# First block: token-major norm sums, another order between a stage's last product and the next norm, conditioning steps moved

## The chip, the cores and the metric

One core of a Trainium2 chip runs the whole program: two transformer blocks after each other on 256 tokens (272 with 16 meta tokens). The metric is the device time of one execution in microseconds (us), the median of the runs; lower is better.

## The reference, cut to what matters

The first block has two layers, each a mixing stage and a conv FFN; the residual h is kept, and the output of each stage is normalised before it is added:

```python
for l in range(DEPTH):                               # first block, DEPTH = 2
    u = _rms_norm(h, norm_mix_pre[l])
    ...
    h = h + _rms_norm(merged @ w_out[l], norm_mix_post[l])
    f = _conv_ffn(_rms_norm(h, norm_ffn_pre[l]), ffn_w_up[l], ffn_conv_w[l], ffn_conv_b[l], ffn_w_down[l])
    h = h + _rms_norm(f, norm_ffn_post[l])

for i in range(DEPTH):                               # second block, on h without the meta tokens
    mod = (cond @ ada_w[i] + ada_b[i]).reshape(bn, N_SUBLAYERS, 3, D_MODEL)
    h = modulate(rms_norm(x, ffn_norm[i, 0]), mod[:, 0, 0], mod[:, 0, 1])
    x = x + 0.5 * mod[:, 0, 2][:, None, :] * swiglu(h, ...)
    ...                                              # a mixer, then a second swiglu, each after such a norm
return rms_norm(x, final_norm)
```

A norm is y * rsqrt(mean(y*y) + 1e-6) * g over the 1024 features of a token. The 144 columns of `mod` (128 features each) are the conditioning.

## The kernel before, in words

Everything lies feature-major: a tensor of 1024 features and 272 tokens is eight tiles (k = 0 to 7) of 128 partitions by 272 columns. Each float32 operand of a big product is split in a high part and a low rest (wh, wl for weights, uh, ul for the activation), and TensorE makes three products per 128 x 128 weight tile: wh*uh, wh*ul, wl*uh (`mm3`). ScalarE writes the high parts (line 114 for weights), VectorE the low ones (line 122). Weights come in one stream of chunks over the SP queue. `prefetch` splits as far ahead as there are buffers: three pairs, one more in the FFNs of the first block, five more in the second block.

The program is written in one order, and each engine works through its own instructions in that order. A stage's products are written out by hand; what follows a product (its eviction) is a generator, which `advance` moves one step after each further product, and `drain` to its end.

**End of a stage of the first block** (`out_gemm`, lines 1470 to 1582; four times, called T1 to T4 below). `evict` squares the product (s[:,0]), scales it to f, and forms s[:,1] = f*f and s[:,2] = h*f; parts 1 to 5 are added into part 0, so three parts are left. `post` needs two norms: r1 of the product, and r2 of the new residual, whose sum of squares follows from that of the old one (`shh`) without a second pass: shh + r1*(2*sum(h*f) + r1*sum(f*f)). It takes column sums over the partitions (line 1527), copies them to SBUF (1533), transposes them (1535), raises them to -1/2 on GpSimd (271), spreads r1 back over the partitions (`spread`), and then sums the other two quantities in the same way. Then, for k = 0 to 7: f*r1 on VectorE (1571), h+f on GpSimd (1573, VectorE for k = 0), the high part of the raw new activation on ScalarE (322), the low one on VectorE (326), with r2 (`second`) computed at k = 2.

**Start of the next stage** (`first_gemm`, line 339, in both blocks). The first group of two to four weight tiles is multiplied with the raw activation, before r2 is known: k is the outer loop, the tiles the inner one. After k = 1 `sums()` is called, after k = 2 r is spread and copied to `pr` (367). After the loop the activation is normalised for all later tiles (`normed`, lines 287 to 309: 302 on VectorE, 304 or 306 on ScalarE, 295 or 297 on VectorE per k), the group's results are multiplied by `pr` (385), and only then do the weight tiles after the next come to be split, where no buffer was free. In the second block `acc_sums` (line 1746) gives token-major sums: the tile of squares is the stationary operand and a column of ones moves through.

**Conditioning.** `ada_step` (line 1713) makes columns of `mod`: one VectorE operation of 128 x 1024 per column and, after every second one, the load of the next two (1 MB, SP queue). Before, each FFN of the first block makes 24 (two per piece of its down product), the swiglus 32, 32, 32 and 0 (one after each up or gate item and each down piece).

Of the kernel before, what the change touches and what calls it, by code (L numbers as in the profile page):

```python
# [9 lines left out]
F32 = mybir.dt.float32  # L10
F32R = mybir.dt.float32r
AF = mybir.ActivationFunctionType
# [6 lines left out]
D = 1024  # L19
KD = 8  # L20
T = 272
META = 16
# [40 lines left out]
class Kern:  # L63
# [190 lines left out]
    def tok_sums(self, sqs, blocks):  # L254


        ps = [self.aps() for _ in blocks]
        for i, s in enumerate(sqs):
            for p, (t0, n) in zip(ps, blocks):
                self.mm(p[:, 0:1], s[:, t0 : t0 + max(n, 128)], self.ones, i == 0, i == len(sqs) - 1)  # L260
        return [p[:, 0:1] for p in ps]
# [51 lines left out]
    def before_norm(self, gain, shift, c, sums):  # L313
# [4 lines left out]
        self.norm = (gain, shift, c, sums)  # L318

    def raw_hi(self, k):  # L320
        gain, _, c, _ = self.norm
        self.nc.scalar.activation(self.uh[:, k, c], self.h[:, k, c], AF.Copy, scale=gain(k))  # L322
# [16 lines left out]
    def first_gemm(self, mk, evict, groups):  # L339
# [11 lines left out]
        for g, size in enumerate(groups):  # L351
            tiles = [(w, *ms[0]) for w, ms in zip(self.get(size), mk[first:])]
            pss = [(self.gps if i < 3 else self.aps)() for i in range(size)]
            self.held = size > 1
            for k in range(KD):
                for (w, m0, m1), ps in zip(tiles, pss):
                    self.mm3(
                        ps[: m1 - m0, : n + c0], w, k, m0, m1, (self.uh, self.ul), k, c.start - c0, n + c0,
                        k == 0, k == KD - 1,
                    )  # L360
                if raw and g == 0 and k == 1:
                    r, bl = sums()
                elif raw and g == 0 and k == 2:
                    ps = self.spread(r, bl)
                    o = c.start if bl[-1][0] > 128 else 0
                    pr = self.wk.tile([128, T], F32, tag="pr", name="pr", bufs=1)[:, :n]
                    nc.scalar.activation(pr, ps[:, o : o + n], AF.Copy)
                elif k in (4, 6):
                    self.prefetch(1)
                    self.advance()  # L370
                yield
# [1098 lines left out]
    def out_gemm(self, w, kt, x, r0, rn, new_f, gname, l, gain, shift=None, mid=None):  # L1470
# [9 lines left out]
        def evict(j, ps):  # L1480
            if j == 0:
                S["f"] = new_f()
            fg = S["f"][:, j, c]
            s = self.s4()
            nc.scalar.activation(s[:, 0, c], ps[:, :rn], AF.Square)
            nc.scalar.activation(fg, ps[:, :rn], AF.Copy, scale=self.v(gname, l * 8 + j))
            S["parts"] = S.get("parts", []) + [s]
            yield
            nc.vector.tensor_tensor(out=s[:, 2, c], in0=self.h[:, j, c], in1=fg, op=MUL)
            nc.scalar.activation(s[:, 1, c], fg, AF.Square)  # L1490
            yield
            if 0 < j < KD - 2:
                acc = S["parts"][0]
                nc.vector.tensor_tensor(out=acc[:, 0:3, c], in0=acc[:, 0:3, c], in1=s[:, 0:3, c], op=ADD)
                S["parts"].remove(s)

        for ch, j0, k0, nk, first, last in self.down_chunks(w, kt):
            def fn(j0=j0, k0=k0, nk=nk, first=first, last=last):
# [18 lines left out]
            if mid is not None:  # L1517
                mid()

        def summed(qs, e, pt):  # L1520

            ps = self.aps()
            n = 32 * len(qs)
            parts = S["parts"]
            for i, src in enumerate(parts):
                for o, q in enumerate(qs):
                    nc.tensor.matmul(
                        ps[32 * o : 32 * o + 32, c], self.ones32, src[:, q, c], start=(i == 0),
                        stop=(i == len(parts) - 1), skip_group_check=True, tile_position=(0, 32 * o),
                    )  # L1530
            if r0:
                nc.vector.memset(e[0:n, 0:r0], 1.0)
            nc.scalar.activation(e[0:n, c], ps[0:n, c], AF.Copy)
            for j, (t0, _) in blocks:
                nc.tensor.transpose(pt[:, n * j : n * j + n], e[0:n, t0 : t0 + 128], self.ident[0:n, 0:n])
            j0, nb = blocks[0][0], len(blocks)
            return pt[:, n * j0 : 3 * n].rearrange("p (b q x) -> p q b x", b=nb, q=len(qs))[:, :, :, 0]

        def post():
# [7 lines left out]
            nb = len(blocks)  # L1547
            pt = self.aps()
            r1 = self.pow_rsqrt(summed([0], self.w1(), pt)[:, 0], nb, D, "r1")[:, :nb]
            self.prefetch(1, ahead=3)  # L1550
            self.drain()
            pt = self.aps()
            sums = summed([1, 2], self.w1(), pt)
            p1 = self.spread(r1, bl)
            f = S["f"]

            def second():
                t = self.sm.tile([128, 4], F32, tag="nt", name="nt", bufs=2)[:, :nb]
                shh = self.shh[:, blocks[0][0] : 3]
                nc.vector.tensor_tensor(out=t, in0=sums[:, 0], in1=r1, op=MUL)  # L1560
                nc.vector.scalar_tensor_tensor(out=t, in0=sums[:, 1], scalar=2.0, in1=t, op0=MUL, op1=ADD)
                nc.vector.tensor_tensor(out=t, in0=t, in1=r1, op=MUL)
                nc.vector.tensor_tensor(out=shh, in0=t, in1=shh, op=ADD)
                return self.pow_rsqrt(shh, nb, D, "r2")[:, :nb]
# [5 lines left out]
            for k in range(KD):  # L1570
                nc.vector.tensor_tensor(out=f[:, k, c], in0=f[:, k, c], in1=p1[:, c], op=MUL)
                eng = nc.gpsimd if k else nc.vector
                eng.tensor_tensor(out=self.h[:, k, c], in0=self.h[:, k, c], in1=f[:, k, c], op=ADD)
                self.raw_hi(k)
                if k == 2:
                    R["r2"] = second()
                if k > 1:
                    self.raw_lo(k - 2)
            self.raw_lo(KD - 2)
# [5 lines left out]
    def conv_ffn(self, l):  # L1585
# [6 lines left out]
        def pool_open():  # L1592
# [3 lines left out]
            self.xp, self.n_spare, self.phase = self.ff, 1, phase  # L1596
            self.ada_begin(range(24 * l, 24 * l + 24))
            S["gh"] = self.ff.tile([128, KF, T], F32R, tag="gh", name="gh", bufs=1)
# [65 lines left out]
    def out_gemm_ff(self, w, S, o0, on, l):  # L1664
# [11 lines left out]
        else:  # L1676
# [3 lines left out]
            lambda: self.ff.tile([128, KD, T], F32, tag="f", name="f", bufs=1), "norm_ffn_post", l, gain, shift,  # L1680
            lambda: self.ada_some(2),
        )
# [67 lines left out]
    def gated_gemm(self, w, kt, x, i, s, half, nxt, order=None, between=None):  # L1750
# [70 lines left out]

        for ch, j0, k0, nk, first, last in self.down_chunks(w, kt):
            def fn(j0=j0, k0=k0, nk=nk, first=first, last=last):
# [17 lines left out]
            self.add(fn, ch)  # L1841
            if kt == KF:
                self.ada_some()

    def swiglu(self, i, s, f, nxt):
# [4 lines left out]
        def pool_open():  # L1850
            self.ff_guard = self.tc.tile_pool(name=f"sw{i}{f}", bufs=1, reuse_waits="tile")
            self.mx = None
            self.ff = self.ph = self.ff_guard.__enter__()
            c = {(0, 0): 48, (0, 2): 80, (1, 0): 112}.get((i, s))
            self.ada_begin(range(c, c + 32) if c else ())
            S["gh"] = self.ff.tile([128, KF, SEQ], F32R, tag="gh", name="gh", bufs=1)
# [564 lines left out]
```

## Time and profile before

| | |
|---|---|
| median of three runs | 2278.74 us (2277.09 to 2283.06) |
| the profiled execution, its own time | 2284.18 us |
| its span, first to last instruction | 2281.6 us |
| granted TensorE clock, mean | 0.978 of full speed |
| TensorE busy with matmuls | 2192.9 us, 96% of the span |
| VectorE, ScalarE, GpSimd busy | 1612.5, 1217.2, 240.6 us |
| DMA | 439.21 MB, mean 192 GB/s |

Matmuls are pipelined, so a busy TensorE isn't yet one at its peak; a matmul row's duration overlaps the next one, and the pace is read from the starts. A wait is put down to what came last.

### The profile page before, as it was taken

The numbers are of one execution on the slowest core, as the hardware profiler recorded it, in microseconds if no ns is written. First come the engines' busy times: TensorE is split into PE (matmuls) and PEld (weight loads), VectorE is DVE, ScalarE is ACT, GpSimd is POOL, SyncE is SP. The second block draws the span as 40 slices with busy tenths as digits, with TensorE's granted clock in tenths as the row PEclk, the third lists the DMA queues.
The fourth block names the chain that finished last, engine by engine and source line by source line (L and its number), as shares of the span: only waits on it lengthen the run. The fifth ranks groups of instructions, "written<-read, shape, count | busy, mean of one in ns | idle before, by whom it ended". The sixth has DMA issues, their size and how long they took to land. (4 is left out here: it accounts for less than half of the span.)

```text
span 2281.6 us, 41972 instructions
## 1 busy us (share of the span) xinstructions
PE 2192.9 (96%) x17048; PEld 2070.0 (91%) x17048; DVE 1612.5 (71%) x2809; ACT 1217.2 (53%) x2221; POOL 240.6 (11%) x285
## 2 busy tenths in 40 slices
PE   7999999999999999999999899986999999999998
PEld 7888888899988798788999799986999999989998
DVE  5655454798885555547989887798877787778553
ACT  4555244577556544445775554465644554466442
POOL 0220111100031001112000100066100000001000
PEclk9999999999999999999999899997999999999999
DMA  7553233454764343324657687733687687744551
GB/s 271 190 183 114 100 102 114 172 206 170 278 242 158 112 148 107 112 97 172 227 184 289 260 302 273 255 111 111 229 283 277 241 303 272 268 174 140 206 177 70
DMA packets 73618, 439.21 MB, mean 192 GB/s; under 512 B 14285, under 2 KB 15629, under 8 KB 25936
## 3 DMA queue, kind: packets, MB, share of 16 engines
q1 hardware_dynamic: 62736, 419.66, 51.3%
q0 software_dynamic: 10400, 16.79, 2.5%
q8 instruction: 133, 2.18, 0.4%
q14 instruction: 61, 0.50, 0.1%
q10 hardware_dynamic: 288, 0.07, 0.0%
HBM read 433.12 MB, written 10.01 MB: 194 GB/s over the span
## 5 line engine op out<-in xcount | busy, mean ns | idle before, releaser
L227 PE MATMUL g<-uh,wh 128*128 128x256 f32 (+2 forms) x3560 | 1034.0, 290 | 18.9 <-ACT uh L322 6.2
L227 PE MATMUL g<-ul,wh 128*128 128x256 f32 (+2 forms) x3560 | 1025.1, 288 | 9.5 <-DVE ul L326 5.9
L227 PE MATMUL g<-uh,wl 128*128 128x256 f32 (+2 forms) x3560 | 1021.8, 287 | 2.7 <-DVE wl L122 2.7
L122 DVE TENSOR_TENSOR wl<-raw,wh 128x1024 fp32r<-128x1024 f32 (+2 forms) x660 | 785.8, 1196 | 274.2 <-ACT wh L114 273.7
L114 ACT ACTIVATE wh<-raw 128x1024 fp32r<-128x1024 f32 (+2 forms) x660 | 670.2, 1020 | 335.5 <-PE g L227 298.9
L227 PEld LDWEIGHTS g<-uh,wh 128*128 128x128 f32 x3560 | 680.1, 191 | 42.2 <-issue 13.5
L227 PEld LDWEIGHTS g<-ul,wh 128*128 128x128 f32 x3560 | 678.7, 191 | 14.0 <-DVE ul L326 6.9
L227 PEld LDWEIGHTS g<-uh,wl 128*128 128x128 f32 x3560 | 680.7, 191 | 3.7 <-DVE wl L122 3.4
L227 PE MATMUL g<-gh,wh 128*128 128x256 f32 (+1 forms) x1056 | 299.2, 283 | 0.0
L227 PE MATMUL g<-gh,wl 128*128 128x256 f32 (+1 forms) x1056 | 299.2, 283 | 0.0
L227 PE MATMUL g<-gl,wh 128*128 128x256 f32 (+1 forms) x1056 | 299.1, 283 | 0.0
L227 PEld LDWEIGHTS g<-gl,wh 128*128 128x128 f32 x1056 | 201.5, 191 | 0.0
L227 PEld LDWEIGHTS g<-gh,wh 128*128 128x128 f32 x1056 | 201.3, 191 | 0.0
L227 PEld LDWEIGHTS g<-gh,wl 128*128 128x128 f32 x1056 | 201.3, 191 | 0.0
L1717 DVE CUSTOM_DVE_ANT_0 adaw<-adaw,condb,vec 128x1024 f32<-128x1024 f32 x144 | 182.4, 1280 | 1.5 <-DMA adaw<-in_ada_t_dram 1.5
L1620 DVE SCALAR_TENSOR_TENSOR y<-edge,vec,y 128x272 f32<-128x272 f32 (+1 forms) x176 | 86.4, 493 | 28.5 <-ACT y L1615 25.4
L227 PE MATMUL g<-oh,wh 128*128 128x272 f32 (+1 forms) x296 | 87.9, 297 | 0.0
L227 PE MATMUL g<-ol,wh 128*128 128x272 f32 (+1 forms) x296 | 84.6, 286 | 0.0
L227 PE MATMUL g<-oh,wl 128*128 128x272 f32 (+1 forms) x296 | 84.5, 285 | 0.0
L1863 ACT ACTIVATE sg<-g 128x256 f32<-128x256 f32 x80 | 30.6, 382 | 99.9 <-PE g L227 99.8
L1224 ACT ACTIVATE gt<-g 128x272 f32<-128x272 f32 (+1 forms) x64 | 25.1, 392 | 107.7 <-PE g L227 107.7
L1252 POOL TENSOR_TENSOR merged<-merged,w 128x272 f32<-128x272 f32 (+1 forms) x48 | 37.9, 798 | 338.5 <-DVE w L1251 338.3
(377 smaller groups left out, 2434.2 us busy)
## 6 DMA issues: line engine op xcount, KB each, us to landing
raw<-in_weights_dram SPq DMA_DIRECT2D x294, 1024.0 KB, 4.9
adaw<-in_ada_t_dram SPq DMA_DIRECT2D x72, 1024.0 KB, 6.6
raw<-in_weights_dram SPq DMA_DIRECT2D x28, 768.0 KB, 4.8
skew<-scr POOLq DMA_DIRECT2D x6, 1086.0 KB, 22.7
h<-skew POOLq DMA_DIRECT2D x8, 544.0 KB, 4.4
h<-skew POOLq DMA_DIRECT2D x8, 512.0 KB, 5.4
condb<-cond SPq DMA_DIRECT2D x5, 512.0 KB, 4.7
hd<-h SPq DMA_DIRECT2D x2, 1088.0 KB, 9.1
```

What stands on the lines that cost most here:

```text
L114: self.nc.scalar.activation(h3[:, :, d0 : d0 + n], c.tile[:, :, c0 : c0 + n], AF.Copy)
L122: self.nc.vector.tensor_tensor(out=l3[:, :, d0 : d0 + n], in0=c.tile[:, :, c0 : c0 + n], in1=h3[:, :, d0 : d0 + n].bitcast(F32), op=SUB,)
L227: self.nc.tensor.matmul(out, lhsT, rhs, start=start, stop=stop, skip_group_check=True)
L1224: nc.scalar.activation(t[:, :rn], ps[:, :rn], AF.Tanh, scale=0.5)
L1252: nc.gpsimd.tensor_tensor(out=mg, in0=mg, in1=t, op=ADD)
L1620: nc.vector.scalar_tensor_tensor(out=y, in0=e[:, o : o + on], scalar=cw(i), in1=y, op0=MUL, op1=ADD)
L1717: self.nc.vector.tensor_tensor_reduce(out=t[:, i, :], in0=t[:, i, :], in1=self.condb, scale=1.0, scalar=self.v("ada_b_2", c), op0=MUL, op1 ...
L1863: nc.scalar.activation(t, ps[:, :SEQ], AF.Silu)
```

## The change

It replaces the column sums, copies and transposes of `post` by token-major sums; puts the first norm's sums ahead of the last eviction's remaining steps and the other two sums behind the spread of r1; adds up to six products of a weight tile that is already split while r1 is computed (`warm`; they write to a PSUM tile that nobody reads); moves `second()` from k = 2 to k = 5 and the low part of k = 0 ahead of it; in `first_gemm` takes wh*uh and wl*uh of all tiles first and then wh*ul of all, and spreads r after k = 5 rather than k = 2; and lets each FFN of the first block make 12 conditioning columns instead of 24, none in its last two pieces, with the rest in the swiglus (40, 32, 40, 8), whose down pieces make two each in the first ten.

```diff
@@ new
+    def warm(self, n):
+        if self.n_used not in self.split_tiles:
+            return
+        ps, w = self.gps(), self.split_tiles[self.n_used][0]
+        for _ in range(n):
+            self.mm(ps[: w.shape[2], :SEQ], w[:, 0, :], self.ul[:, KD - 1, META:T])
@@ first_gemm
-                    self.mm3(
-                        ps[: m1 - m0, : n + c0], w, k, m0, m1, (self.uh, self.ul), k, c.start - c0, n + c0,
-                        k == 0, k == KD - 1,
-                    )
-                if raw and g == 0 and k == 1:
-                    r, bl = sums()
-                elif raw and g == 0 and k == 2:
...
+                    o = ps[: m1 - m0, : n + c0]
+                    self.mm(o, w[0][:, k, m0:m1], self.uh[:, k, t], k == 0, False)
+                    self.mm(o, w[1][:, k, m0:m1], self.uh[:, k, t], False, False)
+                for (w, m0, m1), ps in zip(tiles, pss):
+                    self.mm(ps[: m1 - m0, : n + c0], w[0][:, k, m0:m1], self.ul[:, k, t], False, k == KD - 1)
+                if raw and g == 0:
+                    if k == 1:
+                        r, bl = sums()
+                    elif k == 5:
...
@@ out_gemm, evict
+            if 0 < r0 < META:
+                nc.vector.memset(s[:, 0:3, 0:r0], 1.0)
             nc.scalar.activation(s[:, 0, c], ps[:, :rn], AF.Square)
+            S["parts"] = S.get("parts", []) + [s]
+            if j == KD - 1:
+                yield
             nc.scalar.activation(fg, ps[:, :rn], AF.Copy, scale=self.v(gname, l * 8 + j))
-            S["parts"] = S.get("parts", []) + [s]
@@ out_gemm, post (summed() is gone)
-            pt = self.aps()
-            r1 = self.pow_rsqrt(summed([0], self.w1(), pt)[:, 0], nb, D, "r1")[:, :nb]
+            sums = self.tok_sums([s[:, 0, :] for s in S["parts"]], bl)
+            self.warm(6)
+            self.pipes[0].send(None)
             self.prefetch(1, ahead=3)
+            r1 = self.pow_rsqrt(sums, nb, D, "r1")[:, :nb]
             self.drain()
-            pt = self.aps()
-            sums = summed([1, 2], self.w1(), pt)
             p1 = self.spread(r1, bl)
+            ps = self.aps()
+            for q in range(2):
+                for b, (t0, n) in enumerate(bl):
+                    for i, s in enumerate(S["parts"]):
+                        self.mm(
+                            ps[:, 4 * q + b : 4 * q + b + 1], s[:, 1 + q, t0 : t0 + max(n, 128)], self.ones,
+                            i == 0, i == len(S["parts"]) - 1,
+                        )
...
-                if k == 2:
+                if k == 1:
+                    self.raw_lo(0)
+                elif k > 2:
+                    self.raw_lo(k - 2)
+                if k == 5:
                     R["r2"] = second()
-                if k > 1:
-                    self.raw_lo(k - 2)
@@ conv_ffn, out_gemm_ff, gated_gemm, swiglu
-            self.ada_begin(range(24 * l, 24 * l + 24))
+            self.ada_begin(range(12 * l, 12 * l + 12))
...
-            lambda: self.ada_some(2),
+            lambda n: self.ada_some(2 if n < 2 else 1 if n < 10 else 0),
...
-            if kt == KF:
-                self.ada_some()
+            if kt == KF and n < 10:
+                self.ada_some(2)
...
-            c = {(0, 0): 48, (0, 2): 80, (1, 0): 112}.get((i, s))
-            self.ada_begin(range(c, c + 32) if c else ())
+            self.ada_begin(range(*{(0, 0): (24, 64), (0, 2): (64, 96), (1, 0): (96, 136), (1, 2): (136, 144)}[i, s]))
```

## Rows read from the trace of the kernel before

**Rows 1.** The page's part 1: busy us, share of the span, instructions.

```profile
PE 2192.9 (96%) x17048; PEld 2070.0 (91%) x17048; DVE 1612.5 (71%) x2809; ACT 1217.2 (53%) x2221; POOL 240.6 (11%) x285
```

**Rows 2.** Timeline of PE at T1: start us, us, instructions; in brackets idle before, releaser.

```profile
436.17 1.56 PE L1527 MATMUL a<-s,ones 128*32 128x272 f32 x6
...
440.97 1.03 PE L227 MATMUL a<-ident,r 16*128 16x16 f32 x6
...
445.53 0.59 PE L227 MATMUL g<-ul,wh 128*128 128x272 f32 x1 [1.58 <-DVE ul L326]
...
462.26 0.40 PE L227 MATMUL g<-uh,wl 128*128 128x272 f32 x1 [1.19 <-DVE wl L122]
```

**Rows 3.** Timeline of DVE at T1.

```profile
442.04 0.44 DVE L1571 TENSOR_TENSOR f<-f,a 128x272 f32<-128x272 f32 x1 [1.68 <-PE a L227]
...
443.56 0.15 DVE L1560 TENSOR_TENSOR nt<-a,r 128x3 f32<-128x3 f32 x1
...
453.32 0.91 DVE L302 SCALAR_TENSOR_TENSOR w<-h,vec,pr 128x272 f32<-128x272 f32 x2
...
460.99 2.35 DVE L122 TENSOR_TENSOR wl<-raw,wh 128x1024 fp32r<-128x1024 f32 x2
```

**Rows 4.** Timeline of POOL at T1.

```profile
443.38 1.48 POOL L1573 TENSOR_TENSOR h<-h,f 128x272 f32<-128x272 f32 x2 [3.53 <-DVE f L1571]
445.16 1.04 POOL L271 TENSOR_TENSOR r<-ms,mhalf 128x3 f32<-128x3 f32 x1 [0.30 <-DVE ms L269]
446.17 4.47 POOL L1573 TENSOR_TENSOR h<-h,f 128x272 f32<-128x272 f32 x5
```

**Rows 5.** Timelines of PE, then DVE, at a stage change of the second block.

```profile
1807.40 0.71 PE L227 MATMUL a<-ident,rs 128*128 128x128 f32 x4 [0.39 <-POOL rs L271]
...
1815.14 0.28 PE L227 MATMUL g<-uh,wh 128*128 128x256 f32 x1
...
1808.57 0.88 DVE L302 SCALAR_TENSOR_TENSOR w<-h,gs,pr 128x256 f32<-128x256 f32 x2 [1.78 <-ACT pr L367]
...
1814.49 0.48 DVE L297 SCALAR_TENSOR_TENSOR ul<-w,mod,uh 128x256 fp32r<-128x256 f32 x1
1815.93 0.48 DVE L297 SCALAR_TENSOR_TENSOR ul<-w,mod,uh 128x256 fp32r<-128x256 f32 x1 [0.96 <-ACT uh L306]
```

**Rows 6.** Waits of PE, whole span: us in total, times, longest.

```profile
PE a L227 <- POOL rs L271: 4.2, 7, 1.2
```

**Rows 7.** Timeline of PE, token-major sums of the second block.

```profile
1480.59 0.50 PE L227 MATMUL a<-ones,acc 128*128 128x1 f32 x4
1480.95 0.58 PE L227 MATMUL a<-ones,w 128*128 128x1 f32 x4
```

**Rows 8.** Timelines of PE and DVE at T2, then at T4.

```profile
649.15 1.56 PE L1527 MATMUL a<-s,ones 128*32 128x272 f32 x6
...
655.39 0.44 DVE L1571 TENSOR_TENSOR f<-f,a 128x272 f32<-128x272 f32 x1 [2.58 <-PE a L227]
...
1271.17 0.62 PE L1527 MATMUL a<-s,ones 128*32 128x256 f32 x2 [0.21 <-ACT s L1485]
...
1277.87 0.42 DVE L1571 TENSOR_TENSOR f<-f,a 128x256 f32<-128x256 f32 x1 [0.65 <-PE a L227]
```

**Rows 9.** Conditioning step by line; then busy times (PE, PEld, DVE, ACT, POOL) in a swiglu's down stage.

```profile
L1717 DVE CUSTOM_DVE_ANT_0 adaw<-adaw,condb,vec 128x1024 f32<-128x1024 f32 x144 | 182.4, 1280 | 1.5 <-DMA adaw<-in_ada_t_dram 1.5
...
1420.00:1440.00 20.00, 20.00 (x169) 20.00 (x168) 14.94 (x25) 9.59 (x14) 0.40 (x1) 1.00 0.80 277
```

**Rows 10.** Busy times in stretches (after POOL's: granted clock, DMA share, GB/s).

```profile
444.90:448.60 3.70, 3.07 (x14) 3.07 (x15) 3.69 (x10) 1.57 (x3) 3.44 (x4) 0.54 0.00 0
...
673.60:677.30 3.70, 3.67 (x17) 3.67 (x18) 3.29 (x6) 1.81 (x5) 3.51 (x8) 0.54 0.97 337
...
1076.40:1083.40 7.00, 6.22 (x28) 6.00 (x28) 6.17 (x21) 3.85 (x7) 5.37 (x7) 0.51 0.03 12
...
1291.70:1299.00 7.30, 5.66 (x24) 4.44 (x23) 6.79 (x17) 3.97 (x8) 0.00 (x0) 0.72 0.52 215
```

More of the change, by code (lines that the diff above doesn't have):

```diff
@@ L355, in first_gemm @@
             for k in range(KD):
+                t = slice(c.start - c0, c.stop)
                 for (w, m0, m1), ps in zip(tiles, pss):
-                    self.mm3(
-                        ps[: m1 - m0, : n + c0], w, k, m0, m1, (self.uh, self.ul), k, c.start - c0, n + c0,
-                        k == 0, k == KD - 1,
-                    )
-                if raw and g == 0 and k == 1:
-                    r, bl = sums()
-                elif raw and g == 0 and k == 2:
[L364 to L368, printed above, removed]
+                    o = ps[: m1 - m0, : n + c0]
[7 more added lines that the diff above has]
+                    elif k == 5:
+                        ps = self.spread(r, bl)
+                        o = c.start if bl[-1][0] > 128 else 0
+                        pr = self.wk.tile([128, T], F32, tag="pr", name="pr", bufs=1)[:, :n]
+                        nc.scalar.activation(pr, ps[:, o : o + n], AF.Copy)
+                if k in (4, 6):
                     self.prefetch(1)
@@ L1495, in evict @@
                 S["parts"].remove(s)
-        for ch, j0, k0, nk, first, last in self.down_chunks(w, kt):
+        for n, (ch, j0, k0, nk, first, last) in enumerate(self.down_chunks(w, kt)):
             def fn(j0=j0, k0=k0, nk=nk, first=first, last=last):
@@ L1517, in out_gemm @@
             if mid is not None:
[L1518 to L1537, printed above, removed]
+                mid(n)
         def post():
@@ L1559, in second @@
                 shh = self.shh[:, blocks[0][0] : 3]
-                nc.vector.tensor_tensor(out=t, in0=sums[:, 0], in1=r1, op=MUL)
-                nc.vector.scalar_tensor_tensor(out=t, in0=sums[:, 1], scalar=2.0, in1=t, op0=MUL, op1=ADD)
+                nc.vector.tensor_tensor(out=t, in0=ps[:, 0:nb], in1=r1, op=MUL)
+                nc.vector.scalar_tensor_tensor(out=t, in0=ps[:, 4 : 4 + nb], scalar=2.0, in1=t, op0=MUL, op1=ADD)
                 nc.vector.tensor_tensor(out=t, in0=t, in1=r1, op=MUL)
@@ L1820, in gated_gemm @@
             return
-        for ch, j0, k0, nk, first, last in self.down_chunks(w, kt):
+        for n, (ch, j0, k0, nk, first, last) in enumerate(self.down_chunks(w, kt)):
             def fn(j0=j0, k0=k0, nk=nk, first=first, last=last):
```

## The prediction, made before the changed kernel ran

> **What bounds the kernel now.** I read the page's busy shares first: TensorE (PE) is busy for 96% of the span [rows 1], so PE sets the time and only what stops or slows PE counts. The waits of PE come next: they are short and many, and those that belong to this change lie at nine places. In the first block there are four stage ends (T1 to T4: after the mixing and after the FFN of each of two layers), in the second block five. The timeline shows T1 in full. PE starts the column sums at 436.17 us, gets r1 spread at 440.97, starts the next stage's stream at 445.53 and then has to wait once more, for a low weight half (wl), until 462.26 [rows 2]. What the reader is to see is on VectorE (DVE): from f*p1 at 442.04 it works nearly without a break: residual and raw uh/ul, the normalised uh/ul from 453.32, and only at 460.99 the wl for which PE waits [rows 3]. So at T1 the end of the stage change is not the stream's start at 445.53, but that wl, 26.1 us after the sums began. T2 and T3 have the same form, T4 too, with more weight splits ahead of its normalising.
>
> The pace on that way is GpSimd's (POOL): seven additions h+f and the power for r2 follow each other with only 0.30 us idle, from 443.38 to 450.64 [rows 4]; the last uh, then pr, then the normalising wait for it.
>
> The second block is different. There the spread of r comes after k=2 of the first group (at 1807.40 in the one stage change shown), so DVE normalises beside the group's products, starts at 1808.57, and PE goes from the group's last product into the next tile at 1815.14 with no wait. The one loss is 0.39 us before the spread, alike at all five places [rows 5]; the list of waits has 4.2 us in 7, start and end of the kernel included [rows 6].
>
> **The change, part by part.** Times are from the profiled execution (span 2281.6, its own time 2284.18 us, 5.4 above the median of three runs, 2278.74); a difference found in it is put onto that median.
>
> *Token-major sums, first norm.* Removed: column sums, ACT's copy, the transposes. Added: three parts by three blocks, two passes each, 18 matmuls of one column. Four such start at 1480.59 and the next four at 1480.95, 0.09 us each; the last four take 0.58 with their end, so I take 0.11: 2.0 us [rows 7]. After them come 0.2 hand-over, three small DVE operations (0.3), POOL's power (1.0, as r2 took in rows 4), the spread (1.0, 440.97 to 442.04) and hops (0.2): f*p1 starts 4.7 us after the sums begin. Before, it took 5.87 at T1 (T3, of the same form, is taken like it), 6.24 at T2 and 6.70 at T4 [rows 2, 3, 8]. At T4 there are two blocks (12 matmuls, a shorter spread), so 3.5. Gains of f*p1: T1 and T3 1.15 each, T2 1.55, T4 3.2 us. The larger ones at T2 and T4 hold the conditioning steps that go, 1.28 us each on DVE, two of which stood in its queue there [rows 9].
>
> *The other two sums* move behind the spread: 36 matmuls, 4.0 us of PE in T1 to T3, 24 at T4 (2.7). The stream then starts at 4.7+3.9=8.6 us against 9.36 at T1 (445.53-436.17). This lies beside DVE's and POOL's work, which needs nothing of PE until the normalising. If that cover is gone, it costs up to 4.0 us a place.
>
> *New order on DVE and POOL.* ul(0) no longer waits for second(), which is good for PE's start, but second() now comes after ul(3). POOL's r2 sits between the fifth and sixth addition instead of after the second. From f*p1: first addition +1.3, second and third after it to +3.9, uh(3) and ul(3) on ACT and DVE to +5.1, the five small operations 1.6 (443.56 to 445.16 in rows 3, 4), r2 1.0, two additions of 0.89: the last ends at +9.6. Before, it ended at +8.6 (450.64-442.04). POOL idles meanwhile. So the last addition comes 1.0 us later after f*p1, and pr and the normalising with it. Bounds: 0, if POOL keeps its pace [rows 4], to 1.6, the whole length of second(); a gain is excluded, as nothing leaves this chain. I take 1.0, from the steps.
>
> Net on the chain to wl: T1 and T3 -0.1 each, T2 -0.5, T4 -2.2: together **-2.9 us**. A wait added: second() holds ul(4) to ul(7) behind it, and PE reaches k=4 some 4.5 us after the stream's start, at about +8.4 from f*p1, when ul(4) is just ready; less than 0.5 us, and inside the chain.
>
> *Spread at k=5.* In the first block it costs nothing by itself, as pr waits for the last uh there. In the second block it takes away the cover of the normalising. The group has four tiles, 12 products per k; from the spread to 1815.14 lie 60 products, 0.121 us each beside half a us of the spread. Three k later and without the 0.39 wait, the spread moves from 1807.40 to 1811.4. DVE's first normalising operation follows 1.17 later, at 1812.6. From there the seventh ul began 5.92 later (1814.49); the eighth, one more pass through DVE and ACT behind it, ends 7.0 after the start when PE doesn't hold it back: 1819.6 [rows 5]. PE ends its group at 1814.75 and would end the next tile's 24 products at 1817.6; it now waits for each ul and ends them at 1819.85. Before, it was 1815.14+24*0.12=1818.0. Loss 1.85 us, at four places 7.4. At the fifth, ahead of the conv mixer, DVE's taps follow in the same queue and later hold PE up, so DVE's own delay counts: 1819.6 against 1816.4 (1815.93+0.48), 3.1 us. Together **+10.5 us**. That a late normalising stops PE can be seen at T4 before the change: PE needed 1291.7 to 1299.0, 7.3 us, for 24 products [rows 10]. Bounds: 0 (if something else hides it) to 5*3.1=15.5.
>
> *Conditioning moved.* 24 of 144 columns go from the first block's FFNs to the swiglus: the same loads of 1 MB on SP's queue and steps on DVE [rows 9], one condb load more. In two swiglu down stages the step rate doubles for ten pieces: DVE, busy 14.94 of 20 us there, gets 3.8 steps more (one per piece of 5.3 us), 4.9 us or more: 20 of 20 [rows 9]. Weights split up to eight tiles ahead hide that, and the last two pieces have no step; without that cover it is about one step, 1.3 us, at each of two. I take 0, bounds 0 and 3. The raw loads behind the adaw loads on SP have the same cover.
>
> *Keep-busy products.* Six products of about 0.12 us while PE waits for r1: no cost. Their gain would be a higher clock. The rows show the low level (1.2 GHz) after thin stretches: granted 0.54 at T1 and 0.51 at T3 as the stream starts, 0.54 at T2 right after the wl wait, 0.72 during T4's waits [rows 10]. At T1 to T3 the slow stretch just after the stream starts is hidden: PE waits for the normalising and wl anyway. What counts is the clock when PE restarts from those later waits, and there the change makes PE's stretch thinner (the stream ends earlier, wl does not). I take one more such slow restart as 1.7 us (half of 3.7 at 0.54); bounds -3.7 (both shown ones gone) to +7.
>
> **The sum:** -2.9+10.5+0+1.7 = **+9.3 us**: 2293.5 against the profiled 2284.18, and 2288 against the median.
>
> **The rivals.** (1) *The clock is kept and the chain gets no longer* (faster). All four f*p1 gains reach PE, 7.0 us; the stream's start counts and not wl, which adds the half-clock time: 3.4 us at T1 and 6.9 at T3 lay at the lower clock, T2 and T4 are taken like them, and two restarts had 3.4 and 4.1: half of 28 us is 14. With the second block's +10.5 that is -10.5: 2268. For it: the thin stretches do end in a lower granted clock [rows 10]. Against: the wl wait stands after all of that [rows 2]. The Trainium skill (TensorE: Matmul & The Clock Gate, Part 1) says that the lower clock is the idle default and that activity releases it, so by that page keep-busy products would hold the full clock; the trace agrees that the lower clock follows thin stretches. By that rule alone the sum would be near this rival's. (2) *The f*p1 gains reach PE because second() does not delay POOL, and T2's and T4's restarts keep the clock*: -7.0-3.7+10.5: 2279, no change. It decides if the last addition ends 8.6 us after f*p1 as now. (3) *Products or the spread don't do what they say*: the keep-busy products are skipped when the next tile isn't split yet; that costs and gives nothing here. (4) *The doubled conditioning stalls PE too*, DVE late at the ends of two swiglus: +3 more, 2291; within my range.
>
> **How the numbers follow.** A measurement of this kernel can tell about 0.3%, 6.8 us, from no change. Forecast with (4): 0.57, its own range 2284 to 2296. Rival 2: 0.26. Rival 1: 0.17. Slower by over 0.3% needs more than 2285.6; the forecast's cases lie nearly all above, so 0.56; same 0.27; faster 0.17. The range reaches from rival 1's price to the forecast with more slow restarts, 2268 to 2296.
>
> **What would show it.** Right: POOL's r2 after five additions, with idle time before it; the normalising at T1 and T3 starting at the same distance from the stage's last product as now; in the second block a staircase of PE waits for ul from the normalising, each tile after a group some 1.9 us longer; no wait for POOL's rs there. Wrong: no PE wait after those groups, or T1's wl wait several us earlier. A DVE with idle time between the normalising and wl would also prove me wrong.

## The result, and the profile after

The changed kernel takes 2301.66 us, the median of four runs (2301.01 to 2302.73), against 2278.60 before: ratio 1.0102, 95% interval 1.0086 to 1.0118, **23 us slower**. The sign was predicted, the size was not: 2288 was forecast and 2296 was the upper end.

The page's part 1 of the kernel after (as in [rows 1]):

```profile
PE 2221.8 (97%) x17176; PEld 2100.8 (91%) x17176; DVE 1613.1 (70%) x2820; ACT 1213.2 (53%) x2213; POOL 239.6 (10%) x285
```

TensorE has 128 more instructions and 29 us more busy time. T1 on PE, the timeline of the kernel after (as in [rows 2]):

```profile
427.62 2.06 PE L227 MATMUL a<-ones,s 128*128 128x1 f32 x18
429.55 0.95 PE L227 MATMUL g<-ul,wh 128*128 128x256 f32 x6
431.02 1.76 PE L227 MATMUL a<-ident,r 16*128 16x16 f32 x6 [0.52 <-POOL r L272]
432.57 7.68 PE L227 MATMUL a<-ones,s 128*128 128x1 f32 x36
440.11 0.57 PE L227 MATMUL g<-uh,wh 128*128 128x272 f32 x1
...
448.87 1.03 PE L227 MATMUL a<-ident,r 16*128 16x16 f32 x6
459.30 0.39 PE L227 MATMUL g<-uh,wl 128*128 128x272 f32 x1 [1.19 <-DVE wl L122]
```

The first 18 products take 2.06 us, as forecast. The 36 behind the spread (18 calls; each float32 product shows as two rows) take 7.68 us, not 4.0, and the stream starts only behind them. The windows of the same stretch (the column before the DMA share is the granted clock):

```profile
424.00:428.00 4.00, 4.00 (x36) 4.00 (x34) 3.27 (x4) 2.22 (x5) 0.00 (x0) 1.00 0.46 193
428.00:431.00 3.00, 2.50 (x22) 2.29 (x21) 1.59 (x5) 1.86 (x4) 1.00 (x1) 0.92 0.72 227
431.00:434.00 3.00, 2.98 (x14) 2.94 (x14) 1.53 (x4) 0.24 (x1) 0.00 (x0) 0.50 0.32 128
434.00:437.00 3.00, 3.00 (x16) 3.00 (x15) 2.76 (x7) 1.33 (x3) 2.12 (x3) 0.50 0.00 0
437.00:440.00 3.00, 3.00 (x16) 3.00 (x15) 1.54 (x4) 1.56 (x3) 2.15 (x3) 0.50 0.00 0
440.00:445.00 5.00, 5.00 (x26) 5.00 (x26) 3.97 (x17) 1.65 (x3) 2.52 (x3) 0.58 0.02 6
```

From 431 us to the stream, and for its first 4 us, the granted clock is 0.50, the 1.2 GHz level, although PE's rows are busy nearly throughout (8.98 of 9.00 us from 431 to 440). Who then waits for PE stands in the timelines of VectorE, ScalarE and GpSimd (as in [rows 3, 4]):

```profile
432.81 0.44 DVE L1577 TENSOR_TENSOR f<-f,a 128x272 f32<-128x272 f32 x1 [1.43 <-PE a L227]
440.29 0.16 DVE L1566 TENSOR_TENSOR nt<-a,r 128x3 f32<-128x3 f32 x1 [1.75 <-PE a L227]
450.37 0.92 DVE L303 SCALAR_TENSOR_TENSOR w<-h,vec,pr 128x272 f32<-128x272 f32 x2 [3.76 <-ACT pr L380]
...
449.93 0.40 ACT L380 ACTIVATE pr<-a 128x272 f32<-128x272 f32 x1 [4.58 <-PE a L227]
...
441.32 0.86 POOL L272 TENSOR_TENSOR r<-ms,mhalf 128x3 f32<-128x3 f32 x1 [2.17 <-DVE ms L270]
442.15 1.70 POOL L1579 TENSOR_TENSOR h<-h,f 128x272 f32<-128x272 f32 x2
```

`second()` waits for the 36 products, POOL for `second()`, and `pr` waits 4.58 us for PE, which starts the stream at half speed and reaches its k=5 only at 448.87. At T1 the stage end (first sum to the last wl wait) grows from 26.09 to 31.68 us, at T2 from 24.48 to 29.07, at T3 from 25.36 to 29.73. At T4 (first sum to the first normalising operation) it shrinks from 22.24 to 20.09. (The prediction counted T4 from 1271.17; four of its column products had already run at 1269.90, and from the first of them f*p1 took 7.97, not 6.70.) **Together +12.4 us in the first block**, where -2.9 was forecast.

In the second block, the distance from its first token sums to those of the final norm grows from 791.03 us (1480.59 to 2271.62) to 803.42 (1486.07 to 2289.49): **+12.4**, where +10.5 was forecast. The rows of these sums, of the kernel after, then the last of the kernel before (its first is in [rows 7]):

```profile
1486.07 0.50 PE L227 MATMUL a<-ones,acc 128*128 128x1 f32 x4
...
2289.49 0.61 PE L227 MATMUL a<-ones,acc 128*128 128x1 f32 x4 [0.91 <-DVE acc L1800]
...
2271.62 0.61 PE L227 MATMUL a<-ones,acc 128*128 128x1 f32 x4 [0.91 <-DVE acc L1792]
```

PE's list of waits of the kernel after shows the staircase, and POOL's rs, 4.2 us in 7 waits in [rows 6], down to the two at the ends; below it one step of the staircase in the timeline of PE:

```profile
PE g L227 <- DVE ul L298: 3.9, 23, 0.2
...
PE a L227 <- POOL rs L272: 2.2, 2, 1.2
...
1826.27 0.39 PE L227 MATMUL g<-ul,wh 128*128 128x256 f32 x1 [0.17 <-DVE ul L298]
```

The list adds up to 3.9 us only, since it holds idle time alone and rows overlap: this product is listed with a wait of 0.17 us, but starts 0.45 us after the one before it, where 0.12 is the pace. So the distances, and not the list, tell what the staircase costs.

The two profiled spans differ by less (2299.9 - 2281.6 = 18.3 us), as the execution before had 13.65 us at granted clock 0.50 at 274 to 288 us, ahead of T1, which the one after lacks; at half speed that is 6.8 us, and 24.8 less 6.8 is 18.0. Such stretches come and go from execution to execution of one kernel. So parts are compared below by *stage ends*, the sum of the four distances above (98.2 us before, 110.6 after), and by the *second block's distance*, both from the profiled execution; the median stands beside them. Each ratio is to the kernel before as it ran beside that experiment; its median lay between 2276.4 and 2281.0 us from one set of runs to the next, so a difference between medians of different sets is known to some 5 us only.

### The profile page after: what moved, and what is told of

It reads as the page before. It is cut to its first block, busy times and chain, and to the rows that moved or that the text cites. A ratio compares the mean times of both kernels' runs of the same rounds, so it can differ in the third digit from the quotient of the medians.

```text
span 2299.9 us, 42286 instructions
## 1 busy us (share of the span) xinstructions
PE 2221.8 (97%) x17176; PEld 2100.8 (91%) x17176; DVE 1613.1 (70%) x2820; ACT 1213.2 (53%) x2213; POOL 239.6 (10%) x285
## 4 chain that ended last, share of the span: by engine, by line
PE 75%; issue 12%; DVE 6%; ACT 2%; POOL 1%; POOLq 0%; DVEq 0%; ACTq 0%
PE g L227 63%; PE a L227 10%; DVE wl L122 2%; DVE ct L1962 1%; PE a L670 1%; DVE ul L298 1%; ACT wh L114 1%; DVE w L303 1%; DVE cy L1962 1%; DVE ul L296 0%; PE a L679 0%; PE a L709 0%; ACT uh L307 0%; DVE cg L2080 0%; PE a L933 0%
## 5 line engine op out<-in xcount | busy, mean ns | idle before, releaser
L227 PE MATMUL g<-ul,wh 128*128 128x256 f32 (+3 forms) x3584 | 1006.5, 288 | 9.6 <-DVE ul L298 3.9
L227 PEld LDWEIGHTS g<-uh,wh 128*128 128x128 f32 x3560 | 678.8, 191 | 39.1 <-issue 13.7
L227 PEld LDWEIGHTS g<-ul,wh 128*128 128x128 f32 (+1 forms) x3584 | 669.3, 190 | 22.3 <-DVE ul L298 11.0
```

Of the source, the lines that this page charges most:

```text
L227: self.nc.tensor.matmul(out, lhsT, rhs, start=start, stop=stop, skip_group_check=True)
```

## The experiments

**Column form at the new place.** In `post`, the 18 calls that make the 36 products become the column sums of before (the definition of `summed`, which comes back, is left out):

```diff
-            ps = self.aps()
-            for q in range(2):
-                for b, (t0, n) in enumerate(bl):
-                    for i, s in enumerate(S["parts"]):
-                        self.mm(
...
+            pt = self.aps()
+            sums = summed([1, 2], self.w1(), pt)
```

> The changed kernel, with the second and third sums of the first block again in the column form (12 wide products, ACT's copy, transposes) at their new place behind the spread. Theory A (the 36 one-column products stand ahead of the stream, run at granted clock 0.50 for 7.7 us and hold second(), the stream and pr): the stage ends from sums to the last wl wait, 31.7 (T1), 29.1 (T2), 29.7 us (T3), shrink by 4 to 6 us each, T4's 21.2 by 1 to 3; the time falls from 2301.7 to about 2287 (2284 to 2291). Rival B (the new order alone, second() and the spread after k=5, makes the first block longer): the stage ends keep 29 us or more and the time stays within 3 us of 2301.7.

2297.65 us, ratio 1.0087 (1.0067 to 1.0106). In the profiled execution the stage ends fall to 97.2 us. T1 and T2 fall as A says (25.94 and 24.33), T3 by 3.3 us (26.43), short of its 4 to 6. T4, which A counts up to a later wait of PE, does not shrink (20.51 for 20.09): f*p1 starts there 5.45 us after the first sum instead of 3.29, as VectorE waits 3.25 us for ScalarE. The timeline of PE at T1, then its windows:

```profile
438.00 1.03 PE L227 MATMUL a<-ident,r 16*128 16x16 f32 x6 [0.51 <-POOL r L272]
438.96 1.57 PE L1544 MATMUL a<-s,ones 128*32 128x272 f32 x12
...
460.55 0.59 PE L227 MATMUL g<-uh,wl 128*128 128x272 f32 x1 [1.18 <-DVE wl L122]
...
438.00:441.00 3.00, 2.53 (x18) 1.42 (x18) 1.59 (x4) 0.40 (x2) 0.59 (x1) 1.00 0.31 123
441.00:445.00 4.00, 3.94 (x30) 3.71 (x31) 3.56 (x8) 1.87 (x4) 2.80 (x5) 1.00 0.00 0
```

The median fell by 4 only, to 2297.65, where A said 2284 to 2291. The profiled execution was the fastest of four (2294.6); its clock held at T1, up to the wl wait, and at T2. A later run of the same first block (column form with the early spread, below) shows it falling there.

**Old order, tokens kept.** `second()` after k=2, ul two behind uh, and in the first block the spread after k=2.

```diff
-                    elif k == 5:
+                    elif k == (5 if sums == self.acc_sums else 2):
...
+                if k == 2:
+                    R["r2"] = second()
+                if k > 1:
                     self.raw_lo(k - 2)
-                if k == 5:
-                    R["r2"] = second()
```

> The changed kernel with the token-major sums kept, but second() after the third addition, ul two behind uh and the first block's spread after k=2, as before; the second block's spread stays after k=5. Theory A: the one-column products still end some 12 us after the stage's sums begin, and second() now waits for them in DVE's queue with all ul behind it, so the stage ends do not come back to 26 us: time 2296 to 2306. Rival B: the order was the cause, the stage ends come back to about 26 us and the time falls to about 2287.

2301.93 us, ratio 1.0124 (1.009 to 1.0159), stage ends 106.3 (T1 30.86): 4 us less than after, far from 98. The order alone is not the cause.

**Early spread in the second block.** `elif k == (2 if sums == self.acc_sums else 5)`.

> The changed kernel with the spread after k=2 in the second block alone, k=5 kept in the first. The staircase of waits for ul after each of the five groups goes: the stretches from sums to sums shrink by 1.9 us at three places and by 2.5 to 4 at the two others, 10 to 12 us together, time about 2290 (2288 to 2293). Rival (the staircase only sits where other work would have held PE anyway): less than 4 us, time 2298 or more.

2287.89 us, ratio 1.0058 (1.0032 to 1.0084): 13.8 us less than after. The second block's distance is 790.96, 12.5 us less than after and as before (791.03); the stage ends are 109.4 (T1 to T3 within 0.3 us of after, T4 18.54). Of the staircase, 3.9 us in 23 waits after, one wait is left:

```profile
PE g L227 <- DVE ul L298: 0.2, 1, 0.2
```

The second block's term stands.

**Wide products between.** After each of the 18 calls, `self.mm(ws[: wt.shape[2], :SEQ], wt[:, 0, :], self.ul[:, KD - 1, META:T])`; the result goes to a tile that nobody reads. As a call makes two of the 36, that is 18 wide products and 54 in all, not 72.

> The changed kernel with one wide product (256 columns, result not used) after each of the 36 one-column products. Theory A (one-column products leave TensorE at its lower clock): the granted clock comes back towards 1.0 within the stretch, the 72 products take about 8 us (36 at 0.11 and 36 at 0.12), no longer than the 36 alone at 0.50, the stream starts at the full clock and the time is 2295 to 2303. Rival C (the clock stays low because of the wait for r1 ahead of them, whatever follows): granted clock 0.5 over the whole stretch, 72 products take some 15 us, the time is 2315 or more.

2316.48 us (one run). At T1 the clock stays at 0.50, and the 54 products take 11.5 us:

```profile
434.00:438.00 4.00, 4.00 (x20) 4.00 (x21) 3.76 (x8) 1.72 (x4) 2.62 (x4) 0.50 0.00 0
438.00:442.00 4.00, 4.00 (x19) 4.00 (x20) 1.03 (x3) 1.41 (x3) 1.66 (x2) 0.50 0.00 0
```

A missed on the clock. C has the clock and the time; its 15 us were for 72 products. Its reason, the wait for r1, is tested further below. What the run shows besides is the path: the stream starts 4.0 us later than after at T1 (16.46 against 12.49 from the first sum) and the wl wait comes 3.9 later (35.53 against 31.68), at T2 and T3 3.7 and 3.6. At these places what stands ahead of the stream passes to the end one to one. At T4 the clock falls only near the end of the mixed row, and the stage end keeps (19.86 for 20.09).

**Conditioning alone, on the kernel before.**

> The kernel before with the moved conditioning alone (24 columns from the first block's FFNs to the swiglus, no step in the last pieces). My prediction's term: no cost, within 3 us of the kernel before (2276 to 2279). Rival D (two steps per piece make DVE late at the ends of two swiglus): 3 us or more slower, with waits of PE for DVE at the swiglus' ends.

2279.65 us, ratio 1.0006 (0.9992 to 1.002); second block 791.01. It costs nothing. The stage ends fall from 98.2 to 95.2, nearly all of it at T4 (19.45 for 22.24).

**First sums alone, on the kernel before** (the memset of the unused columns moves to `evict`).

```diff
-            r1 = self.pow_rsqrt(summed([0], self.w1(), pt)[:, 0], nb, D, "r1")[:, :nb]
+            sums = self.tok_sums([s[:, 0, :] for s in S["parts"]], bl)
+            r1 = self.pow_rsqrt(sums, nb, D, "r1")[:, :nb]
...
-            sums = summed([1, 2], self.w1(), pt)
+            cs = summed([1, 2], self.w1(), pt)
+            next(cs)
             p1 = self.spread(r1, bl)
+            sums = next(cs)
```

`summed` is a generator here: the first `next` writes the column products and ACT's copy, the second the transposes.

> The kernel before with two edits: the first norm's sums token-major (18 one-column products, 12 at T4), and r1 spread ahead of the transposes of the other two sums, which keep the column form and their place in the wait for r1. f*p1 comes 1.2 to 1.5 us earlier after the sums at T1 to T3 and some 3 us earlier at T4. Theory A (the chain from f*p1 to wl sets the stage end): each stage end follows, together 5 to 7 us faster. Rival (few column sums ahead of r1 make the stretch thinner, the clock falls and takes it back): f*p1 is earlier but the stage ends are not, and the time stays within 2 us of the kernel before.

2276.48 us, ratio 0.9985 (0.9966 to 1.0004): not told from no change by the runs, though the stage ends fall from 98.2 to 94.0, 4.2 us where A said 5 to 7.

**First sums and conditioning.** The two edits above together.

> The same two edits and the moved conditioning. Without a cost of the conditioning (my term) the time is that of the two edits alone or 1 to 2 us less, as two conditioning steps of 1.28 us leave DVE's queue ahead of the sums at T2 and T4: 5 to 9 us faster than the kernel before. Rival D: 3 us or more behind the two edits alone.

**2269.18 us, ratio 0.9966 (0.9955 to 0.9977): faster than both kernels**, stage ends 89.8, second block 791.02. This is called the fastest version below. Its profiled execution was the slowest of twelve (2278.84), with 23.9 us at granted clock 0.50 ahead of T1. T2 and T4 gain more than in the last run (23.08 for 23.96, 17.85 for 21.14), since no conditioning step stands in VectorE's queue. T1 on PE:

```profile
439.20 2.06 PE L227 MATMUL a<-ones,s 128*128 128x1 f32 x18
441.19 1.57 PE L1529 MATMUL a<-s,ones 128*32 128x272 f32 x12
442.69 1.03 PE L227 MATMUL a<-ident,r 16*128 16x16 f32 x6
...
451.95 1.03 PE L227 MATMUL a<-ident,r 16*128 16x16 f32 x6
463.97 0.39 PE L227 MATMUL g<-uh,wl 128*128 128x272 f32 x1 [1.19 <-DVE wl L122]
```

The wide sums fill the wait for r1: the spread follows them without a gap. The granted clock holds through them and falls at 446.67 us, behind a stretch in which PE was busy for 1.44 of 3.60 us:

```profile
443.00:446.60 3.60, 1.44 (x9) 0.97 (x8) 2.69 (x8) 1.27 (x3) 1.47 (x2) 1.00 0.11 41
```

**Column form and early spread.** The edits of the first and the third experiment on the kernel after.

> The changed kernel with both of the first two edits undone: second and third sums in the column form at the new place, and the second block's spread after k=2. If the two terms are independent, the second block gives back 12 us and the first block 11 to 13 us of PE's stage ends: about 2277, within 4 us of the kernel before. If the time stays over 2284, some third part of the change (the order of second(), the conditioning, the keep-busy products) costs 5 us or more.

2285.72 us, ratio 1.003 (1.0014 to 1.0047), so by the expectation some third part costs. Second block 791.60 (11.8 of its 12.4 us are back), stage ends 103.0 (7.6 of 12.4). What is left follows the clock: here it falls ahead of the column sums, which then take 2.94 us, and T1 to T3 come to 28.43, 26.43 and 27.67, where the same first block had 25.94, 24.33 and 26.43 in the first experiment:

```profile
429.96 0.95 PE L227 MATMUL g<-ul,wh 128*128 128x256 f32 x6
431.43 1.76 PE L227 MATMUL a<-ident,r 16*128 16x16 f32 x6 [0.51 <-POOL r L272]
433.12 2.94 PE L1544 MATMUL a<-s,ones 128*32 128x272 f32 x12
```

**New order in the fastest version.** `second()` after k=5 and the first block's spread after k=5.

> The fastest version so far (2269.2 us; first sums token-major, the other two as columns during the wait for r1, conditioning moved) with the new order of the changed kernel in the first block alone: second() after the sixth uh, ul one place earlier, the first block's spread after k=5. My prediction's term for this order was 1.0 us a stage end (the last POOL addition later), none for the spread: about 2273. Rival: the order costs nothing while the clock is kept, 2268 to 2271. Second rival: it costs 2 us or more a stage end, 2277 or more.

2278.12 us, ratio 1.0004 (0.9989 to 1.0018): 9 us over the fastest version by the medians, 4.6 by the stage ends (94.4: T1 25.84 for 24.77, T2 24.71 for 23.08, T3 25.25 for 24.10, T4 18.64 for 17.85). The time is that of the second rival, the stage ends are those of my 1.0 a place. The rest lies elsewhere: from the first sum of T1 to the sums of the final norm the profile is 8.9 us longer than the fastest version's, 4.6 at the stage ends, 1.3 in the second block and 3.0 between the stage ends. It has stretches of 3.4 us at granted clock 0.50 there that the other lacks, at 860, 1089 and 2044 us. Whether the order brings them is not shown.

**Sums in the stream.** The 36 products and `second()` behind k=1 of the stream.

> The changed kernel with the 36 one-column products (and second() behind them) moved after the second k of the next stage's stream, where wide products stand before and behind them. Theory A (their place ahead of the stream is what costs): the stream starts some 7 us after the sums, second() comes at about 13, wl at 27 to 28 where it was 31.7, 29.1 and 29.7: 6 to 10 us less, 2292 to 2296. On the clock: if one-column products by themselves bring the lower level, the granted clock falls to 0.5 at or right behind them in the stream; if it was the thin stretch from the first sums to the spread, the 36 take about 4 us at 1.0 in the places where the clock has not fallen before them.

2316.13 us, ratio 1.0162 (1.014 to 1.0185), stage ends 120.7: the expectation of the time fell. At T1 PE starts the stream 6.0 us after the first sum, behind a wait of 1.56 us for the raw uh. The clock falls in that wait, and the 36 again take 7.67 us, now behind 18 half-speed products, so the run cannot tell what the 36 alone do to the clock; r2 comes at 18.98 from the first sum and wl at 34.99:

```profile
441.61 0.59 PE L227 MATMUL g<-uh,wh 128*128 128x272 f32 x1 [1.56 <-ACT uh L331]
...
445.86 7.67 PE L227 MATMUL a<-ones,s 128*128 128x1 f32 x36
```

**Thirty keep-busy products, and none.** `self.warm(30)`, and the line left out.

> The changed kernel with 30 keep-busy products in place of 6, 2.6 us more of wide products between the first sums and the spread. If the thin stretch before the spread brings the clock down, it now stays at 1.0: the 36 one-column products take 4 us and not 7.7, the stream starts about 1 us earlier and at the full clock, time 2293 to 2299. If the one-column products themselves do it, the clock falls all the same and the stream comes 2.5 us later at three places: 2306 to 2311.

> The changed kernel without the six keep-busy products. They cover 0.7 of the 1.4 us from the last of the first sums to the spread. If they help the clock, it falls earlier or for longer without them, and the time is 2 us or more above 2301.7; if they do nothing for it, the time is 2300 to 2303, since they lie in a wait.

With none: 2301.66 us (2298.67 to 2304.35), ratio 1.0102 (1.0085 to 1.0119), not told from six; that the medians agree to the hundredth is chance. With thirty: 2303.80, ratio 1.0111 (1.009 to 1.0133), above the 2293 to 2299 of a clock that is kept and below the 2306 to 2311 of one that falls. At T1 the clock now holds, and falls at the end of the 36, with PE busy all the time. The timeline of PE:

```profile
430.05 3.78 PE L227 MATMUL g<-ul,wh 128*128 128x256 f32 x30
433.76 1.03 PE L227 MATMUL a<-ident,r 16*128 16x16 f32 x6
434.62 4.12 PE L227 MATMUL a<-ones,s 128*128 128x1 f32 x36
```

and its windows:

```profile
435.00:437.00 2.00, 2.00 (x21) 2.00 (x20) 1.72 (x4) 0.56 (x2) 0.76 (x1) 1.00 0.00 0
437.00:439.00 2.00, 2.00 (x18) 2.00 (x18) 2.00 (x6) 1.00 (x2) 1.35 (x2) 0.88 0.00 0
439.00:441.00 2.00, 2.00 (x10) 2.00 (x10) 1.93 (x7) 1.05 (x2) 2.00 (x3) 0.50 0.00 0
```

T1 shrinks to 29.36. At T2 and T3 the clock falls within the 36: T2 comes to 28.35, T3 grows to 30.42. The stage ends are 108.7, 1.9 us less than after, and the time does not show it: f*p1 starts 1.5 us later than after at T1 and T2, 2.3 and 2.2 later at T3 and T4. So wide work in the gap puts the fall off, and costs about what it gives.

**The same 36 products with nothing to wait for.** In the fastest version, ahead of the spread, in place of the wide sums.

> The fastest version (2269.2 us) with the 12 wide products, the copy and the transposes of the second and third sums replaced by the 36 one-column products in the same place, right behind the first 18 and ahead of r1's spread, so that PE has no wait from the first sum to the spread. If one-column products by themselves keep the clock up, they take 4.0 us at 1.0, the spread comes 2.5 us later, the stage ends too: 2277 to 2281. If they bring the clock down though PE waits for nothing, the granted clock falls within or right behind them, with a longer stretch at 0.50 at T1 to T3 than the 3.4 to 6.8 us of the fastest version, and the time is 2282 to 2290.

2289.66 us, ratio 1.005 (1.0027 to 1.0073), stage ends 106.2. All 54 one-column products run without a break, and at T1 to T3 the clock falls in their midst (at T4, with 36 in a row, it falls just behind them). The timeline of PE:

```profile
428.89 8.29 PE L227 MATMUL a<-ones,s 128*128 128x1 f32 x54
```

and its windows:

```profile
430.90:432.90 2.00, 2.00 (x18) 2.00 (x17) 1.68 (x4) 0.22 (x1) 1.00 (x1) 0.88 0.96 406
432.90:434.90 2.00, 2.00 (x11) 2.00 (x11) 0.00 (x0) 0.00 (x0) 0.00 (x0) 0.50 0.13 49
434.90:436.90 2.00, 2.00 (x11) 2.00 (x11) 0.00 (x0) 0.00 (x0) 0.00 (x0) 0.50 0.00 0
```

The fastest version has the same 18 products ahead and the wide sums in place of the 36, and its clock held through them. So here the clock fell behind one-column products alone, without a wait. The profile is 23.1 us longer than the fastest version's from the first sum of T1 to the final norm's: 16.4 at the stage ends, 0.3 in the second block, 6.3 between, where it has 13.7 us more at granted clock 0.50.

**Late spread, second block alone.** In the fastest version.

> The fastest version (2269.2 us) with the spread of the second block alone after k=5. By the changed kernel's stretches (2.6, 2.0, 1.9, 3.9 and 2.0 us) and the run that put it back (13.8 us): 10 to 13 us slower, 2279 to 2282, with short waits of PE for ul after each of the five groups. My prediction's term was 10.5.

2281.21 us, ratio 1.0003 (0.9984 to 1.0021): 12.0 us over the fastest version by the medians, 9.7 by the second block's distance (800.75 for 791.02). The kernel before, beside it, was at 2281.0, 2.7 above its median beside the fastest version. The waits of PE for ul are there (3.8 us in 22). The stage ends keep (89.5).

## Why the prediction was right in sign and wrong in size

**Right.** The second block: the mechanism (the normalising loses its cover), 1.85 us a place forecast, 1.98, 1.90 and 1.98 us measured at the three plain ones; 12.4 us in all for 10.5, and 9.7 in the fastest version. The place ahead of the conv mixer gave 2.6 for 3.1 (1.6 in the fastest version); most of the excess lies at the stretch before the final swiglu (88.01 to 91.94, +3.9 for 1.85), where the execution after has 3.4 us at the lower clock; four profiles with the late spread that have none there take 90.2 to 90.6. Conditioning at nothing. f*p1 at 4.43 to 5.19 us at T1 to T3 (4.7 forecast), 3.29 at T4 (3.5). The new order at about 1.0 a place, with equal stretches at the lower clock at T1 to T3 in both kernels compared (3.4, 6.8 and 3.4 us). Of its signs, POOL's r2 behind five additions with idle time before it, the staircase and the missing waits for rs are there; the normalising did not keep its distance (T1 22.75 for 17.15 us from the first sum, T3 21.07 for 16.69). The sign came out by the second block alone: the first was to gain 2.9 us and lost 12.4.

**Wrong, first step: "The other two sums ... 36 matmuls, 4.0 us of PE ... This lies beside DVE's and POOL's work, which needs nothing of PE until the normalising."** The size was taken from one-column products in a dense stream [rows 7]; 36 in a row behind 18 more run at 1.2 GHz and take 7.7 us at T1 and T2, 7.3 at T3. And the cover was thin: `second()` needs these sums, and in the new order it stands ahead of the last two additions. By the prediction's own steps the 36 end 8.6 us after the first sum and `second()` comes at 9.8 (4.7 + 5.1), 1.2 us later; at T1 they ended at 12.6. The last addition ended 16.23 us after the first sum, where the steps gave 14.3. The prediction named this price ("up to 4.0 us a place") and put it into no case; at T1 to T3, on top of 2288, it makes 2300.

**Wrong, second step: "In the first block it costs nothing by itself, as pr waits for the last uh there."** Nine kernels give one rule for T1, read off their rows. The normalising starts at the later of two times: 2.67 us after the end of the last addition, or 1.50 us after the start of r2's spread; and the wl wait comes 8.9 us behind it. The other seven profiles follow it too, within 0.05 us. Times in us from the first sum:

| kernel | last addition ends | spread of r2 | normalising | wl wait |
|---|---|---|---|---|
| before | 14.47 | 14.11 | 17.15 | 26.09 |
| after | 16.23 | 21.25 | 22.75 | 31.68 |
| after, old order | 19.25 | 18.21 | 21.94 | 30.86 |
| after, column form | 14.35 | 14.34 | 17.02 | 25.94 |
| after, column form, early spread in block two | 16.43 | 18.00 | 19.50 | 28.43 |
| after, wide products between | 19.83 | 25.11 | 26.61 | 35.53 |
| fastest version | 13.16 | 12.75 | 15.84 | 24.77 |
| fastest, new order | 13.97 | 15.41 | 16.91 | 25.84 |
| fastest, 36 in place of the wide sums | 18.63 | 18.58 | 21.31 | 30.23 |

Before, the addition bound and the spread had 1.5 us to spare (17.15 - 1.50 - 14.11). After, the spread binds by 3.9 us: it waits in PE's queue behind 36 products and six k of a stream that starts at half speed. With the old order the sums bind in the other way, through `second()` and the additions, which is why undoing the order alone gave back so little.

**Wrong, third step: the clock, beside the keep-busy products (no cost, one more slow restart of 1.7 us).** Six are too few to matter (with none the time was not told from that with six), and the prediction priced the lower clock at restarts behind later waits only, and held it to be hidden ahead of the normalising; it came under the 36, ahead of the stream, on the path. The Trainium skill (TensorE: Matmul & The Clock Gate, Part 1) says that activity releases the clock, and rival 1 took "busy" from that. The run with 54 products does not agree with this reading: PE's rows were busy for 2.00 of every 2 us as the granted clock fell to 0.50.

**The 12.4 us of the first block in steps** (stage ends): 98.2 before; 89.8 with the first sums token-major, the wide sums inside r1's wait and the conditioning moved; 94.4 with the new order (+4.6); 103.0 with the wide sums behind the spread, where they no longer fill r1's wait, and with the keep-busy products and the new order of products and eviction (+8.6); 109.4 with the 36 in their place (+6.4, in two kernels that both spread early in block two); the kernel after itself has 110.6. The last steps depend on the execution. The same first block as at 103.0 had 97.2 in the first experiment, so 5.8 of the 8.6 us go with the clock. Where that execution kept the clock, T1 and T2 came to 25.94 and 24.33, beside 25.84 and 24.71 with the new order alone: the place of the sums, the eviction, the order of products and the keep-busy products cost nothing there by themselves. At T4 1.9 us go with the later f*p1 (5.45 for 3.59). Against the execution that kept the clock the 36 cost 13.4 us (110.6 - 97.2), against the one that lost it 6.4.

**Rivals.** The first was right that the clock counts, but here it fell for longer instead of being kept. The second fails in the row of r2, which waits 2.17 us: the last addition ends 11.0 us after f*p1, not 8.6. The third fails in the six products of T1's timeline, the fourth in the run with the conditioning alone. The range was too short since no case had the clock staying low under busy rows.

## What to carry to other kernels

A product of one column is cheap in a dense stream (0.09 us each in the second block) and dear in a long row: in the row of 54 the granted clock fell to 0.50, and each then took 0.21 us. In the rows each has a full stationary tile of 128*128 for its one column. Fill a wait of TensorE with wide work that is needed anyway, ahead of the short thing it waits for. When a step is put off in another engine's queue, write down its latest harmless time: here the spread had 1.5 us to spare, and it was moved by three k of the stream.

## What the runs showed of the hardware that had not been expected

Granted clock 0.50 with PE's rows busy 2.00 of 2 us, in a row of 54 one-column products; they went from 0.11 to 0.21 us each. One wide product after every two of the 36 did not bring the clock back in the 11.5 us that they took at T1; it came back in the dense stream behind them. Whether it falls at a place changes between executions of the same first block: at T1 it held through the column sums in one profiled execution and fell in another, with 25.94 and 28.43 us. Why some executions have stretches at 1.2 GHz far from these places, such as 274 to 288 us, stays open, and with it whether the 3 to 6 us that two runs lose between their stage ends belong to the edits.
